# The opening of a macaron decoder layer: sums of squares by matmuls, modulation on ScalarE, weight parts on VectorE, seven conditioning rows at another place

## The chip, the cores and the metric

The kernel runs on one core of one Trainium2 chip. The metric is the time of one execution on the device in microseconds (us); of several executions the median is taken. The engines are TensorE (PE in the profile, its weight loads PEld), VectorE (DVE), ScalarE (ACT), GpSimd (POOL) and SyncE (SP), which here issues nearly all transfers.

## The reference

One layer, one sequence of 1024 tokens, width 1024, all in float32. Three sub-layers, each with a norm, a modulation by a conditioning vector c, and a gated residual:

```python
c_act = jax.nn.silu(c)
mods = jnp.split(c_act @ w_ada[l] + b_ada[l], 9, axis=-1)
sh1, sc1, gt1, sh2, sc2, gt2, sh3, sc3, gt3 = mods
h = modulate(rms_norm(x, g_ffn1[l]), sh1, sc1)      # h * (1 + scale) + shift
x = x + 0.5 * gt1[:, None, :] * swiglu(h, w1_gu[l], w1_down[l])
h = modulate(rms_norm(x, g_mix[l]), sh2, sc2)
...                                                 # gated convolution and windowed attention
h = modulate(rms_norm(x, g_ffn2[l]), sh3, sc3)
x = x + 0.5 * gt3[:, None, :] * swiglu(h, w2_gu[l], w2_down[l])
return rms_norm(x, g_final)
```

The feed-forward width is 2816, 22 blocks of 128. The change is in the first norm, its modulation and the first three of these blocks, and in when the rows of mods are made.

## The kernel before

Activations lie transposed: a tile holds 128 channels (db, 0 to 7) by 512 tokens (half h, 0 or 1). To keep float32 precision a product is three matmuls of operands split in a high part (the value rounded to the matmul format, written by ACT) and a low part (the rest, by subtraction): `mm3` issues high x high at L138, weight-high x activation-low at L140 and weight-low x activation-high at L142. `split` makes a weight's parts, cast at L106, subtraction at L107.

The opening, inside an order written out by hand for all engines, goes like this. The first half of x is loaded, 8 tiles. `Stats` squares each tile on ACT (L312, L315), adds the squares up on DVE (L319), and then four matmuls with a column of ones (L328) sum over the channels. `rstd_of` makes the inverse root, `spread` (L269) brings it to all partitions, and ACT copies it to sp (L642). Then eight steps, one for each db: DVE multiplies x by the norm and by the scale factor (L275), ACT adds the shift and rounds, giving the high part (L279), DVE makes the low part (L290), ACT writes the full value over x (L285). Between them stand the two rows of mods, shift and scale, that the next step needs: `ada_block` (L225) multiplies a 128 x 1024 block of w_ada by silu(c) and sums it on DVE, and `ada_done` (L235) makes g * (1 + scale). Six weight tiles (gate and up of blocks 0 to 2, w0[0] to w0[5]) are split meanwhile, their subtractions on POOL. `first_mm` issues the matmuls of a step with the tiles that are there. The second half of x gets the same sums, s1, during the last two steps, and then its own pass, `first_h`, with 144 matmuls behind it. That is the end of the hand-written order; PE's order is written out for the whole program.

Then `gu_seven` computes the other 19 blocks by a scheme with seven products in place of eight (L195), `down_seven` the down projection in 10 blocks with POOL adding into x, and the mixing stage follows. The other 56 rows of mods, `steps`, are taken by `some_ada`: seven ahead of `gu_seven`, one for each of its blocks, and the rest in the mixing stage. The order of DVE, ACT and SP outside the opening is set by a scheduler, and it put the seven rows among the sums of the second half. Weights and these rows are loaded through one ring of four buffers (wr, L114), and SP issues in order, so a load that waits for a buffer holds back those behind it.

## Time and profile before

| | |
|---|---|
| median of 3 runs | 2302.0 us (2300.78 to 2303.47) |
| the profiled execution | 2298.75 us, span 2296.8 |
| PE busy | 2210.1 us, 96% of the span |
| DVE busy | 1677.2 us, 73% |
| ACT busy | 1060.4 us, 46% |
| POOL busy | 394.4 us, 17% |

The span is what the profiler saw between the first and the last instruction. A row of the timeline gives start and length in us, engine, line, operation, what it writes and reads, how many of them were merged, and in brackets how long the engine had been idle and what ended that. A row of a group gives busy time and mean length in ns, and idle time before them. Lines are those of the kernel before; in the changed one they are about 10 to 60 higher.

### The profile page before, as it was taken

The numbers are of one execution on the slowest core, as the hardware profiler recorded it, in microseconds if no ns is written. First come the engines' busy times: TensorE is split into PE (matmuls) and PEld (weight loads), VectorE is DVE, ScalarE is ACT, GpSimd is POOL, SyncE is SP. The second block draws the span as 40 slices with busy tenths as digits, with TensorE's granted clock in tenths as the row PEclk, the third lists the DMA queues.
The fourth block names the chain that finished last, engine by engine and source line by source line (L and its number), as shares of the span: only waits on it lengthen the run. The fifth ranks groups of instructions, "written<-read, shape, count | busy, mean of one in ns | idle before, by whom it ended". The sixth has DMA issues, their size and how long they took to land.

```text
span 2296.8 us, 30100 instructions
## 1 busy us (share of the span) xinstructions
PE 2210.1 (96%) x10392; PEld 1849.1 (81%) x10392; DVE 1677.2 (73%) x2966; ACT 1060.4 (46%) x2095; POOL 394.4 (17%) x445
## 2 busy tenths in 40 slices
PE   5899999999998999999899997999999999999997
PEld 3688888888887888888889996788888888888886
DVE  8997778867868777777477776555786777676875
ACT  4554444444446443343476555124644444454442
POOL 3000000006451000000343442002100000002644
PEclk9999999999999999999999998999999999999998
DMA  8265456599732543454121115354233553399922
GB/s 319 76 220 180 149 176 211 193 404 297 262 121 97 183 131 109 155 156 156 55 64 56 52 44 217 131 177 149 69 124 121 184 185 122 119 342 335 351 79 74
DMA packets 146744, 381.63 MB, mean 166 GB/s; under 512 B 20384, under 2 KB 22560, under 8 KB 146592
## 3 DMA queue, kind: packets, MB, share of 16 engines
q1 hardware_dynamic: 141984, 371.33, 46.2%
q0 software_dynamic: 4608, 8.39, 2.1%
q8 instruction: 81, 1.33, 0.2%
q14 instruction: 71, 0.58, 0.1%
HBM read 270.61 MB, written 109.05 MB: 165 GB/s over the span
## 4 chain that ended last, share of the span: by engine, by line
PE 87%; DVE 7%; issue 2%; DMA 2%; ACT 2%; POOL 1%; SPq 0%; DVEq 0%; POOLq 0%; ACTq 0%
PE ps L195 60%; PE ps L142 6%; PE ps L138 6%; PE ps L140 6%; PE ps L977 2%; PE ps L975 2%; PE ps L976 2%; DVE w L107 1%; PE ps L1031 1%; PE ps L1074 1%; DVE t L225 1%; DMA wr<-in_w2d_dram 1%; DMA wr<-in_wada_dram 1%; PE ps L1010 1%; PE ps L1098 1%
## 5 line engine op out<-in xcount | busy, mean ns | idle before, releaser
L195 PE MATMUL ps<-t,w 128*128 128x512 f32 x6468 | 1469.1, 389 | 4.8 <-DVE r L405 3.6
L195 PEld LDWEIGHTS ps<-t,w 128*128 128x128 f32 x6468 | 1213.4, 188 | 260.1 <-DVE r L405 6.2
L106 ACT CAST w<-wr 128x512 fp32r<-128x512 f32 (+1 forms) x420 | 254.9, 612 | 482.4 <-PE ps L195 366.4
L107 DVE TENSOR_TENSOR w<-wr,w 128x512 fp32r<-128x512 f32 (+1 forms) x404 | 304.6, 760 | 137.8 <-ACT w L106 136.3
L515 POOL TENSOR_TENSOR x<-x,g 128x512 f32<-128x512 f32 x96 | 145.1, 1526 | 1060.1 <-DVE x L569 586.2
L106 ACT CAST w<-ws 128x512 fp32r<-128x512 f32 x231 | 143.5, 621 | 251.7 <-PE ps L195 202.1
L140 PE MATMUL ps<-t,w 128*128 128x512 f32 (+1 forms) x528 | 206.9, 392 | 4.9 <-DVE t L290 4.9
L107 DVE TENSOR_TENSOR w<-ws,w 128x512 fp32r<-128x512 f32 x231 | 161.7, 703 | 39.4 <-ACT w L106 38.9
L138 PE MATMUL ps<-t,w 128*128 128x512 f32 (+1 forms) x400 | 158.4, 396 | 6.3 <-ACT t L279 6.2
L142 PE MATMUL ps<-t,w 128*128 128x512 f32 (+1 forms) x400 | 155.9, 390 | 2.0 <-DVE w L107 2.0
L140 PEld LDWEIGHTS ps<-t,w 128*128 128x128 f32 x528 | 102.0, 193 | 27.1 <-DVE t L290 7.6
L344 DVE TENSOR_TENSOR x<-x,x 128x512 fp32r<-128x512 f32 x161 | 102.7, 685 | 2.9 <-ACT x L343 2.7
L343 ACT CAST x<-x 128x512 fp32r<-128x512 f32 x161 | 88.7, 621 | 19.4 <-DVE x L431 12.1
L225 DVE CUSTOM_DVE_ANT_0 wr<-wr,crow_act,v 128x1024 f32<-128x1024 f32 x56 | 71.7, 1282 | 35.1 <-DMA wr<-in_wada_dram 35.0
L138 PEld LDWEIGHTS ps<-t,w 128*128 128x128 f32 x400 | 78.1, 195 | 23.5 <-ACT t L279 9.0
L142 PEld LDWEIGHTS ps<-t,w 128*128 128x128 f32 x400 | 78.0, 195 | 17.3 <-DVE w L107 2.4
L107 POOL TENSOR_TENSOR w<-wr,w 128x512 fp32r<-128x512 f32 (+1 forms) x16 | 21.5, 1355 | 401.5 <-ACT w L106 401.5
L569 DVE SCALAR_TENSOR_TENSOR x<-ps,mods,x 128x512 f32<-128x512 f32 (+1 forms) x104 | 72.6, 707 | 23.9 <-PE ps L195 12.5
L319 POOL TENSOR_TENSOR s<-s,q 128x512 f32<-128x512 f32 (+1 forms) x48 | 56.7, 1184 | 192.1 <-ACT q L315 190.5
L975 PE MATMUL ps<-w,t 128*128 128x384 f32 x256 | 88.3, 345 | 0.0
L977 PE MATMUL ps<-w,t 128*128 128x384 f32 x256 | 85.7, 335 | 0.0
L976 PE MATMUL ps<-w,t 128*128 128x384 f32 x256 | 85.6, 334 | 0.0
(150 smaller groups left out, 2810.5 us busy)
## 6 DMA issues: line engine op xcount, KB each, us to landing
t<-hs SPq DMA_DIRECT2D x140, 512.0 KB, 9.8
hs<-x SPq DMA_DIRECT2D x277, 256.0 KB, 4.5
wr<-in_wada_dram SPq DMA_DIRECT2D x56, 512.0 KB, 3.7
wr<-in_w1gu_dram SPq DMA_DIRECT2D x44, 512.0 KB, 4.5
wr<-in_w2gu_dram SPq DMA_DIRECT2D x44, 512.0 KB, 3.6
wr<-in_wbcu_dram SPq DMA_DIRECT2D x24, 512.0 KB, 4.1
wr<-in_w1d_dram SPq DMA_DIRECT2D x22, 512.0 KB, 7.5
wr<-in_w2d_dram SPq DMA_DIRECT2D x22, 512.0 KB, 7.4
```

What stands on the lines that cost most here:

```text
L106: nc.scalar.copy(hi, src)
L107: lo_engine.tensor_tensor(lo, src, f32(hi), op=ALU.subtract)
L138: mm(o, wh, xh, start=start, stop=False)
L140: mm(o, wh, xl, start=False, stop=False)
L142: mm(o, wl, xh, start=False, stop=stop)
L195: mm(o, a, b, start=first, stop=last, skip_group_check=True)
L225: nc.vector.tensor_tensor_reduce(out=st, in0=st, in1=crow_act, scale=1.0, scalar=v[:, C_BADA + i : C_BADA + i + 1], op0=ALU.mult, op1=ALU. ...
L344: nc.vector.tensor_tensor(f32r(t), t, f32(hi), op=ALU.subtract)
L515: nc.gpsimd.tensor_tensor(dst, dst, r, op=ALU.add)
L975: mm(o[:, :384], xh, wh, start=k == 0, stop=False)
L976: mm(o[:, :384], xh, wl, start=False, stop=False)
L977: mm(o[:, :384], xl, wh, start=False, stop=k == KT - 1)
```

## The change

It does four things. First, the squares of each tile go to PE at once: `BankStats` has four matmuls with the column of ones for each of the eight tiles, adding up in PSUM, and DVE adds nothing. Second, DVE's product holds only the norm and the gain g, and ACT applies scale and shift in one operation, twice (rounded, and full over x); 1 + scale is made on ACT, and the low part is now full minus high. Third, the low parts of the six first weight tiles are made by DVE and not POOL, half a tile (512 columns) at a time, each half where it is first needed. Fourth, the seven rows ahead of `gu_seven` are not taken there, so each of the 56 moves seven places later, and `down_seven` takes one in each of its 10 blocks. Loads and matmuls are reordered to go with this.

```diff
+    class LateWeights(Weights):
+        def __init__(self, raw, tiles):
+            self.half, self.raw = HALF, raw
+            self.t = tiles or [parts_tile() for _ in range(2)]
+        def make(self, i):
+            split(*pair_of(self.t[i]), self.raw[:, i * HALF : (i + 1) * HALF])
...
+    class BankStats:
+        def __init__(self):
+            self.pt, self.n = None, 0
+        def add(self, src):
+            q = scratch("q")
+            nc.scalar.activation(q, src, AF.Square)
+            if self.pt is None:
+                self.pt = bank()
+            for b in range(NB // 2):
+                mm(self.pt[:, b : b + 1], q[:, b * P : (b + 1) * P], ones,
+                   start=self.n == 0 and b == 0, stop=True, skip_group_check=True)
+            self.n += 1
+        def rstd(self):
+            return rstd_of(self.pt[:, 0 : NB // 2], NB // 2, "n")
...
+        def first_u(db, h):
+            u = scratch("u")
+            nc.vector.scalar_tensor_tensor(
+                out=u, in0=xT[db][h], scalar=v[:, C_G1 + db : C_G1 + db + 1], in1=sp,
+                op0=ALU.mult, op1=ALU.mult,
+            )
+            return u
+        def first_hi(u, db, h):
+            for dst in (hh[db][h], xT[db][h]):
+                nc.scalar.activation(
+                    dst, u, AF.Identity, bias=mods[:, db : db + 1],
+                    scale=amod[:, db : db + 1],
+                )
+        def first_lo(db, h):
+            nc.vector.tensor_tensor(
+                hl[db][h], xT[db][h], f32(hh[db][h]), op=ALU.subtract)
...
             ada_block(crow_act, m, db, sta.pop(0))
             if m == 1:
-                ada_done(m, db, 1)
+                nc.scalar.activation(
+                    amod[:, db : db + 1], mods[:, 8 + db : 9 + db], AF.Identity, bias=ones)
...
-            u = modulated_hi(xT[db][0], sp, 0, db, hh[db][0])
+            first_hi(first_u(db, 0), db, 0)
             if db + 1 < KT:
                 first_ada(db + 1, 0)
-            modulated_lo(u, 0, db, hh[db][0], hl[db][0])
-            modulated_full(u, 0, db, xT[db][0])
+            first_lo(db, 0)
...
-        def first_w(i):
-            w0[i] = Weights(w0[i], 1024, nc.gpsimd, [tile_t(), tile_t()] if i > 3 else None)
+        def first_w(i, part):
+            if part == 0:
+                w0[i] = LateWeights(w0[i], [tile_t(), tile_t()] if i > 3 else None)
+            w0[i].make(part)
...
-        s0 = Stats(engine=nc.vector)
+        s0 = BankStats()
...
         first_step(7)
-        for db in range(2, KT):
+        s1 = BankStats()
+        for db in range(KT):
             s1.add(xT[db][1])
         first_mm((7,), 0, (0, 1, 2, 3, 4))
         r1 = s1.rstd()
...
-        some_ada(7)
         gu_seven(w1gu, range(3, NJ), hid, ts, lambda to: some_ada(1))
...
-        down_seven(w1d, hid, gate, ngate, xT, x_block)
+        down_seven(w1d, hid, gate, ngate, xT, x_block, lambda: some_ada(1))
```

What moves on the engines, at the three places that count. On PE at the start of the program (s and q are squares, nr the inverse root, t_113 the first channel block, w its weights), before:

```order
L328 MATMUL ps_267<-ones,s_219 128x1 x4
L269 MATMUL ps_292<-ident,nr_273 128x128 x4
L138 MATMUL ps_304<-t_113,w_283 128x512
L140 MATMUL ps_304<-t_113,w_283 128x512
L142 MATMUL ps_304<-t_113,w_283 128x512
L138 MATMUL ps_305<-t_113,w_298 128x512
```

and with the change:

```order
L355 MATMUL ps_221<-ones,q_219 128x1 x4
L355 MATMUL ps_221<-ones,q_226 128x1 x4
L355 MATMUL ps_221<-ones,q_232 128x1 x4
L355 MATMUL ps_221<-ones,q_238 128x1 x4
L355 MATMUL ps_221<-ones,q_244 128x1 x4
L355 MATMUL ps_221<-ones,q_250 128x1 x4
L355 MATMUL ps_221<-ones,q_256 128x1 x4
L355 MATMUL ps_221<-ones,q_262 128x1 x4
L279 MATMUL ps_313<-ident,nr_294 128x128 x4
L148 MATMUL ps_319<-t_113,w_304 128x512
L150 MATMUL ps_319<-t_113,w_304 128x512
```

One group of sums has become eight, one for each tile of squares. On DVE in the second step (u is the scaled block, t_244 to t_262 and t_278 to t_284 are rows of mods), before:

```order
L290 SCALAR_TENSOR_TENSOR t_113<-u_314,mods,t_113 128x512
L225 ISA t_252,mods<-t_252,crow_act,v 128x1024
L225 ISA mods 128x1
L235 SCALAR_TENSOR_TENSOR amod<-mods,v 128x1
L275 SCALAR_TENSOR_TENSOR u_338<-x_98,amod,spr_291 128x512
L225 ISA t_256,mods<-t_256,crow_act,v 128x1024
L225 ISA mods 128x1
L290 SCALAR_TENSOR_TENSOR t_114<-u_338,mods,t_114 128x512
```

and with the change, first DVE, then ACT beside it:

```order
L692 TENSOR_TENSOR t_113<-x_97,t_113 128x512
L235 ISA t_278,mods<-t_278,crow_act,v 128x1024
L235 ISA mods 128x1
L107 TENSOR_TENSOR w_333<-wr_274,w_333 128x512
L107 TENSOR_TENSOR w_343<-wr_280,w_343 128x512
L678 SCALAR_TENSOR_TENSOR u_351<-x_98,v,spr_312 128x512
L235 ISA t_282,mods<-t_282,crow_act,v 128x1024
L235 ISA mods 128x1
L692 TENSOR_TENSOR t_114<-x_98,t_114 128x512
```

```order
L686 ACTIVATE t_113<-u_325,mods,amod 128x512
L686 ACTIVATE x_97<-u_325,mods,amod 128x512
L705 ACTIVATE amod<-mods,ones 128x1
L106 CAST w_333<-wr_274 128x512
L106 CAST w_343<-wr_280 128x512
L686 ACTIVATE t_114<-u_351,mods,amod 128x512
L686 ACTIVATE x_98<-u_351,mods,amod 128x512
```

Weight subtractions (L107) have come between a row of mods and the next product, and the small product L235 on DVE has become L705 on ACT, ahead of the casts that these subtractions need. On PE near the end of the eight steps (t_119 and t_120 are the last two blocks, ps_564 and ps_543 the second half's sums, t_492 the sixth weight tile), before:

```order
L138 MATMUL ps_307<-t_120,w_359 128x512
L140 MATMUL ps_307<-t_120,w_359 128x512
L142 MATMUL ps_307<-t_120,w_359 128x512
L138 MATMUL ps_308<-t_120,t_395 128x512
L140 MATMUL ps_308<-t_120,t_395 128x512
L142 MATMUL ps_308<-t_120,t_395 128x512
L328 MATMUL ps_564<-ones,s_498 128x1 x4
L138 MATMUL ps_309<-t_113,t_492 128x512
L140 MATMUL ps_309<-t_113,t_492 128x512
L142 MATMUL ps_309<-t_113,t_492 128x512
```

and with the change:

```order
L148 MATMUL ps_323<-t_119,t_444 128x512
L150 MATMUL ps_323<-t_119,t_444 128x512
L152 MATMUL ps_323<-t_119,t_444 128x512
L355 MATMUL ps_543<-ones,q_541 128x1 x4
L355 MATMUL ps_543<-ones,q_548 128x1 x4
L355 MATMUL ps_543<-ones,q_554 128x1 x4
L355 MATMUL ps_543<-ones,q_560 128x1 x4
L355 MATMUL ps_543<-ones,q_566 128x1 x4
L355 MATMUL ps_543<-ones,q_572 128x1 x4
L355 MATMUL ps_543<-ones,q_578 128x1 x4
L355 MATMUL ps_543<-ones,q_584 128x1 x4
L148 MATMUL ps_319<-t_120,w_305 128x512
```

The 15 matmuls of t_120 stood ahead of the sums; now they stand behind all eight groups of them.

More of the change, by code (lines that the diff above doesn't have):

```diff
@@ L643, in first_spread @@
             return sp
+        def first_u(db, h):
[14 more added lines that the diff above has]
+                hl[db][h], xT[db][h], f32(hh[db][h]), op=ALU.subtract)
         def first_h(dbs, h):
-            us = [modulated_hi(xT[db][h], sp, 0, db, hh[db][h]) for db in dbs]
+            us = [first_u(db, h) for db in dbs]
             for u, db in zip(us, dbs):
-                modulated_lo(u, 0, db, hh[db][h], hl[db][h])
-            for u, db in zip(us, dbs):
-                modulated_full(u, 0, db, xT[db][h])
+                first_hi(u, db, h)
+            for db in dbs:
+                first_lo(db, h)
         def first_ada(db, m):
@@ L709, in tile_macaron_layer @@
         first_ada(0, 1)
-        first_w(0)
-        w0[4] = load_st(w1gu[2, 0])
+        first_w(0, 0)
+        first_ada_load(4)
         sp = first_spread(r0)
-        first_w(1)
         first = {(i, 0): bank() for i in range(6)}
-        first_ada_load(4)
         first_step(0)
+        first_w(1, 0)
         first_mm((0,), 0, (0, 1))
-        first_w(2)
+        first_w(2, 0)
         first_ada_load(5)
@@ L722, in tile_macaron_layer @@
         first_mm((0, 1), 0, (2,))
-        first_w(3)
+        first_w(3, 0)
         first_ada_load(6)
@@ L727, in tile_macaron_layer @@
         first_mm((0, 1, 2), 0, (3,))
-        first_w(4)
+        first_w(0, 1)
+        w0[4] = load_st(w1gu[2, 0])
         first_ada_load(7)
-        w0[5] = load_st(w1gu[2, 1])
         load_x(1)
@@ L733, in tile_macaron_layer @@
         first_mm((3,), 0, (0, 1, 2, 3))
+        first_w(1, 1)
+        first_w(4, 0)
+        w0[5] = load_st(w1gu[2, 1])
         first_mm((0, 1, 2, 3), 0, (4,))
         first_step(4)
-        first_mm((4,), 0, (0, 1, 2, 3, 4))
+        first_mm((4,), 0, (0, 1))
+        first_w(2, 1)
+        first_mm((4,), 0, (2,))
         first_step(5)
-        first_mm((5,), 0, (0, 1, 2, 3, 4))
-        first_w(5)
-        s1 = Stats(engine=nc.vector)
+        first_mm((5,), 0, (0, 1, 2))
+        first_w(3, 1)
+        first_mm((4, 5), 0, (3,))
         first_step(6)
-        for db in range(2):
-            s1.add(xT[db][1])
-        first_mm((6,), 0, (0, 1, 2, 3, 4))
+        first_w(4, 1)
+        first_mm((6,), 0, (0, 1, 2, 3))
+        first_mm((4, 5, 6), 0, (4,))
         first_step(7)
-        for db in range(2, KT):
+        s1 = BankStats()
+        for db in range(KT):
             s1.add(xT[db][1])
@@ L749, in tile_macaron_layer @@
         r1 = s1.rstd()
+        first_w(5, 0)
         first_sw(0, 0)
-        first_mm((0, 1, 2), 0, (5,))
+        first_w(5, 1)
+        first_mm((0, 1, 2, 3), 0, (5,))
         sp = first_spread(r1)
-        first_mm((3, 4, 5, 6, 7), 0, (5,))
+        first_mm((4, 5, 6, 7), 0, (5,))
         first.update({(i, 1): bank() for i in range(6)})
```

## The prediction

> **What bounds the kernel now.** I read the busy time by stage first, then TensorE's waits, then the timeline of the stage that the change touches. Columns of the first view: stretch and length, then busy time (instructions) of PE, PEld, DVE, ACT and POOL, granted PE clock, DMA share, GB/s.
>
> ```profile
> 20.00:30.00 10.00, 3.29 (x6) 1.78 (x6) 9.54 (x12) 4.46 (x8) 7.41 (x4) 1.00 1.03 410
> ...
> 60.00:70.00 10.00, 4.76 (x19) 3.11 (x17) 9.21 (x16) 4.46 (x8) 0.00 (x0) 0.98 0.53 160
> ...
> 80.00:90.00 10.00, 10.00 (x48) 8.36 (x48) 8.43 (x13) 6.78 (x11) 0.00 (x0) 1.00 0.01 2
> ...
> 540.00:560.00 20.00, 20.00 (x90) 16.55 (x89) 19.75 (x23) 8.31 (x14) 14.12 (x14) 1.00 1.02 314
> ```
>
> From 80 us PE is full, and still is at 540 to 560, in the first down projection. Before 80 us it is a third to a half busy and DVE is full. So the change is worth what it does to one moment: the end of the opening, after which PE has only work in a row. PE's waits up to 165 us agree; the third row is from the chain of waits:
>
> ```profile
> PE ps L328 <- DVE s L319: 22.3, 2, 13.7
> ...
> PE ps L195 <- DVE r L405: 0.7, 1, 0.7
> ...
> 116.74 13.37 PE ps L195 x59
> ```
>
> The two long ones stand before the group of matmuls that adds up each half's squares (13.7 and 8.6 us). I therefore follow the opening to the end of the second half's 144 matmuls: L195, the next stage, starts at 116.74 now. In a row a matmul takes 13.37 / 59 = 0.227.
>
> **Part 1, the first sums on TensorE.** Now:
>
> ```profile
> 6.56 0.61 ACT L312 ACTIVATE s<-x 128x512 f32<-128x512 f32 x1
> ...
> 8.30 3.98 ACT L315 ACTIVATE q<-x 128x512 f32<-128x512 f32 x6 [0.61 <-DMA x<-in_x_dram]
> ...
> 13.68 1.78 PEld L328 LDWEIGHTS ps<-ones,s 128*128 128x128 f32 x8 [13.68 <-DVE s L319]
> 13.69 1.87 PE L328 MATMUL ps<-ones,s 128*128 128x1 f32 x8 [13.69 <-DVE s L319]
> ...
> 15.59 0.26 ACT L253 ACTIVATE nt<-ps,eps 128x4 f32<-128x4 f32 x1 [2.01 <-PE ps L328]
> ...
> 16.36 0.16 DVE L259 TENSOR_TENSOR nt<-nt,nv 128x4 f32<-128x4 f32 x1
> 16.56 1.16 DVE L260 SCALAR_TENSOR_TENSOR nr<-nt,nr 128x4 f32<-128x4 f32 x1
> ...
> 20.57 0.75 DVE L275 SCALAR_TENSOR_TENSOR u<-x,amod,spr 128x512 f32<-128x512 f32 x1 [0.36 <-ACT spr L642]
> ```
>
> One group of four instructions runs as eight records with a fresh weight load each: 1.78 us for eight loads, about 0.213 apiece, 1.71 a group. The change removes seven DVE adds, but PE now does eight such groups instead of one. ScalarE delivers squares every 0.66 us, so PE is the slower: from 7.17 (6.56 + 0.61) it needs 8 x 1.71 = 13.7, to 20.9 instead of 15.56. **+5.3.** That is PE's slow clock; with the fast one a group costs:
>
> ```profile
> 688.10 1.05 PE L328 MATMUL ps<-ones,s 128*128 128x1 f32 x8 [0.31 <-POOL s L319]
> ```
>
> about 0.86 in a row. Does the burst itself raise the clock? Five stretches, cut where the granted clock changes in steps of about 3.41 us:
>
> ```profile
> 694.24:697.65 3.41, 3.41 (x10) 2.62 (x9) 3.26 (x5) 2.47 (x5) 0.21 (x1) 0.50 0.34 132
> 697.65:711.30 13.65, 8.87 (x39) 6.44 (x38) 13.64 (x17) 10.05 (x18) 5.01 (x3) 1.00 0.27 97
> 711.30:714.72 3.42, 3.42 (x11) 2.92 (x12) 0.73 (x5) 0.26 (x1) 0.00 (x0) 0.50 0.00 0
> 714.72:718.13 3.41, 3.41 (x9) 2.64 (x8) 0.00 (x0) 0.00 (x0) 0.00 (x0) 0.50 0.00 0
> 718.13:721.50 3.37, 3.37 (x20) 2.89 (x19) 0.00 (x0) 0.00 (x0) 0.00 (x0) 1.00 0.00 0
> ```
>
> In the first, third and fourth PE is busy without a gap at half clock. One such window of 512-column matmuls was enough to lift the clock at 697.65; the window from 711.30, whose first 0.8 us were one-column matmuls of this line, did not lift it, and it took the next one. So one-column matmuls count for less than they last, and a stretch of nothing else should stay slow: I take 20.9.
>
> The Trainium skill, "TensorE: Matmul & The Clock Gate", Part 1, says that whatever is issued in the first 3.4 us or so runs slow and everything after it fast, without asking which matmuls; by that the burst would end near 16.3. The window from 711.30 speaks against it.
>
> **Part 2, from the sums to the first block.** Now 15.56 to 20.57, 5.0 us, of which 1.0 is the last small DVE operation stretched by a running POOL subtraction (1.16 against the 0.16 before it). After: activation 0.3, five small DVE operations 0.9, then on ACT the scale's addition (behind ada row two: 1.3, itself near the 0.26 above), a 0.6 cast and the 0.6 copy of the spread, then DVE's half-tile subtraction 0.6: 4.1. **-0.9.** The first scaled block starts near 24.95.
>
> **Part 3, the eight steps.** An undisturbed step now, its ACT part and the last one's, a scale stretched by POOL, the prices of cast and subtraction; the second row is from the chain of waits, the last two are POOL's group and a load's time to land:
>
> ```profile
> 44.64 0.75 DVE L275 SCALAR_TENSOR_TENSOR u<-x,amod,spr 128x512 f32<-128x512 f32 x1
> ...
> 45.39 1.20 DVE t L225
> ...
> 45.43 0.73 ACT L279 ACTIVATE t<-u,mods 128x512 fp32r<-128x512 f32 x1 [2.72 <-DVE u L275]
> 46.06 0.71 ACT L285 ACTIVATE x<-u,mods 128x512 f32<-128x512 f32 x1
> ...
> 60.66 0.71 ACT L285 ACTIVATE x<-u,mods 128x512 f32<-128x512 f32 x1
> ...
> 48.70 0.75 DVE L275 SCALAR_TENSOR_TENSOR u<-x,amod,spr 128x512 f32<-128x512 f32 x1
> ...
> 33.59 1.73 DVE L275 SCALAR_TENSOR_TENSOR u<-x,amod,spr 128x512 f32<-128x512 f32 x1
> ...
> 36.60 1.12 ACT L106 CAST t<-wr 128x512 fp32r<-128x512 f32 x2
> ...
> 100.18 1.90 DVE L107 TENSOR_TENSOR t<-x,t 128x512 fp32r<-128x512 f32 x3
> ...
> L107 POOL TENSOR_TENSOR w<-wr,w 128x512 fp32r<-128x512 f32 x6 | 10.9, 1838 | 5.0 <-ACT w L106 5.0
> ...
> wr<-in_w1gu_dram SPq DMA_DIRECT2D x44, 512.0 KB, 4.5
> ```
>
> A step is 4.06 alone and about 6.0 with POOL at work; all, from 20.57 to the end of the last block's second ACT pass at 61.37, take 40.8. Taking the subtractions off POOL ends the stretching, worth about a microsecond in each of some ten DVE operations. The price: on DVE a step becomes scale 0.67, ada 1.2, low part 0.6, ada 1.2, weight subtraction 0.6, so 4.28. And two new waits. The low part now needs ACT's second pass: 0.75 + 0.62 + 0.72 from the scale's start against 0.67 + 1.2 of DVE work, 0.3 late. The weight subtraction needs a cast that stands on ACT behind the scale's addition, which needs the second ada row: 0.1 + 0.2 + 0.62, with hand-over 0.98, in which DVE does nothing and the next scale is queued behind. 5.56 a step. Six steps 33.3, two steps with a second subtraction 1.2, the last one with three sums of the next weights queued ahead 6.5, two ACT passes 2.1: 43.2. **+2.4** (bounds: no cast wait, -3.5; steps as long as the stretched ones, +5).
>
> The DMAs have slack. The fifth tile's load and with it the last ada pair and the second half of x wait on SP until the first tile's second subtraction has freed a buffer, near 24.95 + 3 x 5.56 + 0.6 = 42. They hold 3.7 MB, so 9 us at the 410 GB/s of the first view, and 4.5 us to land: there by 56; the ada pair is needed at 60 and the half at 68.
>
> **Part 4, the second sums and the seven rows.** Now, first one of DVE's groups between 61.4 and 73.7, then PE:
>
> ```profile
> L225 DVE CUSTOM_DVE_ANT_0 wr<-wr,crow_act,v 128x1024 f32<-128x1024 f32 x7 | 8.9, 1280 | 0.0
> ...
> 73.65 1.87 PE L328 MATMUL ps<-ones,s 128*128 128x1 f32 x8 [8.60 <-DVE s L319]
> 75.38 0.77 PE L138 MATMUL ps<-t,t 128*128 128x512 f32 x1
> ...
> 79.37 1.28 PE L269 MATMUL ps<-ident,nr 128*128 128x128 f32 x8
> 80.41 0.48 PE L138 MATMUL ps<-t,t 128*128 128x512 f32 x1
> ```
>
> The sums end at 75.38, 14.0 after the ACT pass (61.37), the seven rows' 8.4 us among them; both go from here. After: the first square is ready 0.6 behind the pass, at 68.7, and PE's eight groups follow: 6.9 at the fast clock. But they last over two of the 3.41 us windows, so one is filled with one-column matmuls alone; I take it that the clock falls, on average 5.1 us in, and the last 2.1 groups cost 1.71: 8.7, end at 77.4. 9.3 in place of 14.0: **-4.7** (-6.5 if the clock stays).
>
> **Part 5, what PE has left then.** The last block's 15 matmuls now come behind the sums and no more ahead of them: 39 before the second half and not 24, 15 x 0.227 = **+3.4.** Slow ones: today nine (75.38 to 79.37, a loss of 1.95); afterwards until a whole window is filled, 5.1 us on average, a loss of 2.55: **+0.6.** The second half's first low part follows the copy of the spread, two scales and two ACT passes (0.6 + 1.4 + 1.4), with only 12 matmuls, 2.7, as cover: **+0.7.**
>
> Sum: 5.3 - 0.9 + 2.4 - 4.7 + 3.4 + 0.6 + 0.7 = **+6.8 us**; PE would reach the next stage near 123.5 and not 116.7.
>
> **Part 6, the ten rows that land in the down projection.** 10 x 1.2 us DVE and ten loads in a stage with PE full. They cost nothing while the weights there stay ahead; what covers them is that a block's weights are prepared most of a block of 19 us ahead:
>
> ```profile
> 577.53 0.69 DVE L154 TENSOR_TENSOR ws<-wr,wr 128x512 f32<-128x512 f32 x1 [3.41 <-DMA wr<-in_w1d_dram]
> ...
> 601.92 0.75 DVE L569 SCALAR_TENSOR_TENSOR x<-ps,mods,x 128x512 f32<-128x512 f32 x1
> ```
>
> The first sum for a block's weights is at 577.5; its third product leaves PSUM at 601.9, so PE began it some 9.5 us (42 matmuls) before, near 592. DVE is at 19.75 of 20 in the stretch from 540: without that cover 1.2 to 2.3 each, at most about 20. I take 0; less than nothing is excluded, since PE has no wait there to remove. Three rows fewer in the mixing stage: 0, no wait of PE there names L225.
>
> The profiled execution took 2298.75 (span 2296.8), below the runs' median of 2302.0. Profile 2305.6, so the median **2309**.
>
> **Rivals.**
> A, the other side: **the burst raises the clock.** The squares' groups count as work, so the first burst speeds up after one window. Counted back 201 windows from 694.24, one runs from 8.17 to 11.58; by then 2.6 groups are done, and 5.4 at 0.86 end at 16.3 (+0.7). The second burst never slows (-6.5), and no slow matmuls follow it (-1.95). 0.7 - 0.9 + 2.4 - 6.5 + 3.4 - 1.95 + 0.7 = -2.2: 2300, no change. For it: the weight loads keep PE occupied (2.92 of 3.42 in the window from 711.30). Against: that window did not lift the clock. It decides if the first window that the burst fills lifts it.
> B, **slow at the start, fast at the second sums**: a one-column window is too weak to lift the clock but enough to hold it. 6.8 - 1.8 - 2.55 = +2.5: 2304.5, within the noise. The window 697.65 to 711.30 fell only after nearly 3 us of idleness.
> C, **DVE never waits for the casts** (-5.9) on top of A: 2294, faster. Against: the order on ACT puts the cast behind the addition in each step.
> D, **the down projection loses its cover**, +8 on the forecast: 2317. For it 19.75 of 20; against, a whole block of lead.
>
> **Chances.** Forecast 0.58, A 0.12, B 0.13, C 0.10, D 0.07. Under 0.2% (4.6 us) cannot be told from no change. Faster: C and a little of A, 0.13; same: the rest of A, B and the forecast's lower edge, 0.27; slower 0.60. Range 2298 to 2317, holding A, B and D; the forecast's own is 2304 to 2314.
>
> **What would show it.** Right: the 64 records of the first sums end near 21 and the first scale starts near 25; DVE idle about a microsecond before each L107; the second sums start near 69; granted clock 0.5 inside or right behind them; L205 starts near 123. Wrong: first sums done by 17, or L205 before 117; or new PE waits between 480 and 680.

## The result and the profile after

| | before | changed |
|---|---|---|
| median of 4 runs each | 2301.39 us (2297.54 to 2303.47) | 2314.83 us (2311.41 to 2318.73) |
| ratio of the times | | 1.0068, 95% interval 1.0056 to 1.0080 |
| the profiled execution's span | 2296.8 us | 2309.6 us |

The change makes the kernel 13.4 us slower by the medians, 13 to 18 us by the ratio's interval, where +7 was forecast. Two executions of kernels further down, of 3421 us (casts_first) and 7811 us (sums2_early), were slow ones and stand in no ratio. Cutting both profiled executions at the same four places shows where. The third and fourth columns are the times of a stage in us. (The next stage starts at 116.58 in the timeline of the kernel before; the prediction's 116.74 is the row of the chain.)

| from, to | how it is read | before | changed | difference |
|---|---|---|---|---|
| start, next stage | start of the first seven-product matmul | 116.58 | 127.13 | +10.55 |
| gate and up | to the first scaled copy `g<-ps` on ACT | 365.66 | 364.39 | -1.27 |
| down projection | to the end of its last seven-product matmul | 189.24 | 196.93 | +7.69 |
| all that follows | to the end of the span | 1625.3 | 1621.2 | -4.2 |

The last row is not the change's doing. In the sixteen profiles of this study that stretch takes 1621.2 to 1630.8 us, whatever was edited ahead of it, with slow windows of PE's clock at other places each time. So one profile's total is uncertain by some 5 us, and what an edit does is read from the cut at its own stage.

The busy time by stage of the changed kernel, in the stretches that the prediction showed (same columns: PE, PEld, DVE, ACT, POOL, granted PE clock, DMA share, GB/s):

```profile
20.00:30.00 10.00, 4.87 (x14) 3.23 (x14) 7.06 (x15) 4.50 (x9) 0.00 (x0) 1.00 1.03 410
60.00:70.00 10.00, 8.14 (x31) 5.66 (x31) 7.80 (x13) 4.65 (x8) 0.00 (x0) 0.93 0.35 105
80.00:90.00 10.00, 10.00 (x40) 8.47 (x40) 2.63 (x8) 3.16 (x5) 0.00 (x0) 0.73 0.20 52
540.00:560.00 20.00, 17.36 (x69) 13.62 (x69) 12.98 (x20) 6.51 (x11) 10.49 (x10) 0.91 0.84 206
```

The row at 80 to 90 is of the kind that was forecast: PE is full, but behind the second sums its clock is 0.73. The last row speaks against the forecast: at 540 to 560, in the first down projection, PE has lost 2.6 of 20 us although DVE, which was at 19.75, is now at 12.98: idle as well, not overworked. The timeline of the opening (start, length, engine, line, operation; in brackets the idle time before and what ended it; L355 are the one-column sums, L678 the scale, L692 the low part, L686 the pass on ACT, L205 the next stage):

```profile
6.43 13.81 PE L355 MATMUL ps<-ones,q 128*128 128x1 f32 x64 [6.43 <-ACT q L351]
...
24.32 0.75 DVE L678 SCALAR_TENSOR_TENSOR u<-x,v,spr 128x512 f32<-128x512 f32 x1
...
33.03 0.69 DVE L692 TENSOR_TENSOR t<-x,t 128x512 fp32r<-128x512 f32 x1 [0.45 <-ACT x L686]
...
35.80 0.69 DVE L107 TENSOR_TENSOR w<-wr,w 128x512 fp32r<-128x512 f32 x1 [0.87 <-ACT w L106]
36.41 0.74 DVE L678 SCALAR_TENSOR_TENSOR u<-x,v,spr 128x512 f32<-128x512 f32 x1
...
42.19 0.74 DVE L678 SCALAR_TENSOR_TENSOR u<-x,v,spr 128x512 f32<-128x512 f32 x1
...
68.41 0.80 ACT L686 ACTIVATE x<-u,mods,amod 128x512 f32<-128x512 f32 x1
...
69.78 12.14 PE L355 MATMUL ps<-ones,q 128*128 128x1 f32 x64 [0.91 <-ACT q L351]
...
127.13 8.10 PE L205 MATMUL ps<-t,w 128*128 128x512 f32 x35
```

The first sums take 13.81 us for 64 records, 0.216 each, slow to the end. From 36.41 to 42.19 is a step: 5.77 us, with DVE idle 0.45 before the low part and 0.87 before the weight subtraction. The second sums last 12.14 us. And in the down projection, PE's waits from 470 to 690 us (total, times, longest):

```profile
PE ps L205 <- DVE x L599: 2.1, 3, 1.2
PE ps L205 <- ACT w L106: 2.1, 1, 2.1
...
PE ps L205 <- DVE w L107: 0.5, 1, 0.5
```

The DVE and PE rows at the longest of them, in the timeline:

```profile
550.67 0.68 DVE L164 TENSOR_TENSOR ws<-wr,wr 128x512 f32<-128x512 f32 x1
...
552.05 0.73 PE L205 MATMUL ps<-t,w 128*128 128x512 f32 x2 [2.09 <-ACT w L106]
```

And a wait of SP's queue in the same stretch:

```profile
SPq L114 <- DVE mods L235: 37.6, 8, 11.6
```

and the same queue in the kernel before, from 460 to 672 us:

```profile
SPq L114 <- DVE w L107: 95.0, 19, 15.2
```

A block's first weight sum (L164) runs at 550.67, and 1.4 us later PE starts on what was cast from it, 2.09 us late. Before, PE had no such wait. SP waited for a buffer of the ring before as well, 95.0 us, but then for weights to be split; now 37.6 us of its waits are for conditioning rows to be used up before it can issue a load into their buffers.

### The profile page after: what moved, and what is told of

It reads as the page before. It is cut to its first block, busy times and chain, and to the rows that moved or that the text cites. A ratio compares the mean times of both kernels' runs of the same rounds, so it can differ in the third digit from the quotient of the medians.

```text
span 2309.6 us, 30301 instructions
## 1 busy us (share of the span) xinstructions
PE 2235.4 (97%) x10504; PEld 1870.6 (81%) x10504; DVE 1663.9 (72%) x2956; ACT 1065.0 (46%) x2103; POOL 376.4 (16%) x433
## 4 chain that ended last, share of the span: by engine, by line
PE 89%; DVE 4%; DMA 2%; ACT 2%; issue 2%; POOL 1%; SPq 0%; DVEq 0%; POOLq 0%; ACTq 0%
PE ps L205 62%; PE ps L152 6%; PE ps L150 6%; PE ps L148 6%; PE ps L1033 2%; PE ps L1035 2%; PE ps L1034 2%; PE ps L1089 1%; PE ps L1132 1%; DMA t<-in_wada_dram 1%; DVE w L107 1%; DMA x<-in_x_dram 1%; PE ps L1068 1%; PE ps L355 1%; PE ps L1156 1%
## 5 line engine op out<-in xcount | busy, mean ns | idle before, releaser
L205 PE MATMUL ps<-t,w 128*128 128x512 f32 x6468 | 1471.0, 389 | 7.1 <-DVE r L435 2.3
L205 PEld LDWEIGHTS ps<-t,w 128*128 128x128 f32 x6468 | 1214.3, 188 | 263.3 <-DVE r L435 4.2
L107 DVE TENSOR_TENSOR w<-wr,w 128x512 fp32r<-128x512 f32 (+1 forms) x412 | 308.5, 756 | 129.4 <-ACT w L106 128.0
L150 PE MATMUL ps<-t,w 128*128 128x512 f32 (+1 forms) x528 | 208.0, 394 | 6.8 <-DVE t L692 5.6
L107 DVE TENSOR_TENSOR w<-ws,w 128x512 fp32r<-128x512 f32 x231 | 164.6, 716 | 35.1 <-ACT w L106 34.7
L148 PE MATMUL ps<-t,w 128*128 128x512 f32 (+1 forms) x400 | 159.6, 399 | 6.3 <-ACT t L686 4.9
L150 PEld LDWEIGHTS ps<-t,w 128*128 128x128 f32 x528 | 102.5, 194 | 30.0 <-DVE t L692 9.0
L235 DVE CUSTOM_DVE_ANT_0 wr<-wr,crow_act,v 128x1024 f32<-128x1024 f32 x56 | 73.8, 1318 | 35.4 <-DMA wr<-in_wada_dram 35.2
L148 PEld LDWEIGHTS ps<-t,w 128*128 128x128 f32 x400 | 78.4, 196 | 24.1 <-ACT t L686 6.8
L595 ACT ACTIVATE g<-ps,mods 128x512 f32<-128x512 f32 x80 | 55.0, 687 | 57.6 <-PE ps L205 45.6
```

Source lines behind the costliest of these rows:

```text
L107: lo_engine.tensor_tensor(lo, src, f32(hi), op=ALU.subtract)
L148: mm(o, wh, xh, start=start, stop=False)
L150: mm(o, wh, xl, start=False, stop=False)
L205: mm(o, a, b, start=first, stop=last, skip_group_check=True)
```

## The experiments

All ratios are to the kernel before, run beside it on the same chip, with 95% intervals; the changed kernel's is 1.0068 (1.0056 to 1.0080). Where no other kernel is named, the edit is made to the changed kernel. The theory after the first look was that three costs add up: slow one-column matmuls in both sums, waits in the steps, and weights that come late in the down projection.

| run | first scale | next stage | down projection | ratio |
|---|---|---|---|---|
| before | 20.57 | 116.58 | 189.24 | 1 |
| changed | 24.32 | 127.13 | 196.93 | 1.0068 (1.0056 to 1.0080) |
| rows_only | 20.39 | 109.52 | 200.32 | 1.0019 (1.0011 to 1.0027) |
| rows_in_gu | 24.54 | 125.71 | 189.24 | 1.0041 (1.0030 to 1.0053) |
| ring5 | 24.83 | 129.20 | 189.24 | 1.0032 (1.0020 to 1.0044) |
| sums1_back | 19.44 | 122.22 | 197.69 | 1.0066 (1.0053 to 1.0079) |
| sums2_back | 24.54 | 120.28 | 197.67 | 1.0050 (1.0038 to 1.0062) |
| sums2_mixed | 24.95 | 125.10 | 197.40 | 1.0066 (1.0041 to 1.0090) |
| sums2_early | 24.79 | 119.98 | 196.94 | 1.0046 (1.0034 to 1.0057) |
| casts_first | 24.62 | 120.34 | 196.82 | 1.0060 (1.0036 to 1.0084) |
| low_parts_only | 20.28 | 116.56 | 189.24 | 0.9989 (0.9981 to 0.9998) |
| before_rows_gu | 20.58 | 111.02 | 189.24 | 0.9970 (0.9958 to 0.9982) |
| low_parts_casts | 19.01 | 108.35 | 189.24 | 0.9966 (0.9952 to 0.9979) |
| combined | 19.01 | 117.50 | 189.25 | 0.9975 (0.9965 to 0.9986) |
| early_all | 19.38 | 108.30 | 189.24 | 0.9958 (0.9945 to 0.9970) |
| wide_between | 36.83 | 139.61 | 197.45 | one run, 2328.4 us |

### The rows

**rows_only** edits the kernel before:

```diff
-        some_ada(7)
...
-        down_seven(w1d, hid, gate, ngate, xT, x_block)
+        down_seven(w1d, hid, gate, ngate, xT, x_block, lambda: some_ada(1))
```

> The kernel before with only the seven conditioning rows moved, as the change does (none ahead of the gate-and-up stage, one more after each block of the first down projection). Theory T (the moved rows alone make the down projection about 7.7 us longer, since the three loads of a block share four buffers and the sums of the next weights come late on DVE): from the first scaled copy to the last seven-product matmul of the down projection +6 to +9 us, new TensorE waits there for DVE or ACT. In the opening the second sums lose seven rows of 1.2 us ahead of them on DVE: TensorE's wait of 8.60 us before them shrinks, -4 to -7. Sum: 2300 to 2306. Rival R1 (the down projection got longer because everything arrives 10 us later than its transfers, not because of the rows): the down projection keeps its length, and the whole is 2294 to 2298.

The down projection takes 200.32, 11.1 us longer and above the 6 to 9 of the theory; R1 is out. The opening gains 7.06 us: the second sums start at 67.9 and not at 73.65. Together +4.0, and the ratio says +4.4 (0.19% of 2297). So the rows' move is two effects of opposite sign, and the good one is as large as the whole forecast.

**rows_in_gu** takes the rows elsewhere:

```diff
-        gu_seven(w1gu, range(3, NJ), hid, ts, lambda to: some_ada(1))
+        gu_seven(w1gu, range(3, NJ), hid, ts, lambda to: some_ada(2 if len(steps) > 42 else 1))
...
-        down_seven(w1d, hid, gate, ngate, xT, x_block, lambda: some_ada(1))
+        down_seven(w1d, hid, gate, ngate, xT, x_block)
```

> The changed kernel with the seven rows neither ahead of the gate-and-up stage nor in the down projection, but as a second row in its first seven blocks. T: the down projection gets back the length it had before (-7 us against the changed kernel), the gate-and-up stage pays 0 to 3 us for seven rows of 1.2 us on a DVE that is busy 78% there: 2306 to 2311. R1: as long as the changed kernel, 2313 to 2317.

The stage's first scaled copy and last products in the timelines, first of the changed kernel, then of this one:

```profile
491.52 0.69 ACT L595 ACTIVATE g<-ps,mods 128x512 f32<-128x512 f32 x1
...
639.73 48.72 PE L205 MATMUL ps<-t,w 128*128 128x512 f32 x213
```

```profile
490.10 0.69 ACT L595 ACTIVATE g<-ps,mods 128x512 f32<-128x512 f32 x1
...
639.73 39.62 PE L205 MATMUL ps<-t,w 128*128 128x512 f32 x173
```

639.73 + 39.62 - 490.10 = 189.25, within a hundredth of what it was before, against 196.93. The gate-and-up stage pays nothing: 364.39 in both. The ratio falls by 0.27%, 6.2 us.

**ring5** keeps the rows in the down projection and gives the ring a fifth buffer (two other pools give up one buffer each to make room; those lines are left out here):

```diff
-        st = wgt.tile([P, 1024], F32, tag="wr", name=nm("wr"), bufs=4)
+        st = wgt.tile([P, 1024], F32, tag="wr", name=nm("wr"), bufs=5)
```

> The changed kernel with five buffers and not four for the tiles into which weights and conditioning rows are loaded (and, to make room, seven scratch tiles and not eight, and one buffer for the negated gates). Theory T (three loads of a block share four buffers, so a load of the next weights waits for the sums of this block's, and DVE gets to them late): the down projection falls from 196.9 to 189 to 191 us, 2306 to 2309. Rival R4 (DVE is simply full there, ten rows of 1.3 us more than it can take): it stays at 195 to 200 us, the time within 2 us of the changed kernel.

189.24 again, with the same ten rows and the same work on DVE: R4 is out. PE's only wait from 470 to 690 us in this kernel is one that the kernel before has too:

```profile
PE ps L205 <- DVE r L435: 0.8, 1, 0.8
```

DVE's first sum for the weights of the same block (the fourth such sum from 455 us on) stands here in its timeline:

```profile
532.96 0.68 DVE L164 TENSOR_TENSOR ws<-wr,wr 128x512 f32<-128x512 f32 x1
```

and in the kernel before the stage's first scaled copy and the same sum here:

```profile
482.24 0.69 ACT L565 ACTIVATE g<-ps,mods 128x512 f32<-128x512 f32 x1
...
517.56 0.68 DVE L154 TENSOR_TENSOR ws<-wr,wr 128x512 f32<-128x512 f32 x1
```

Counted from the first scaled copy of the stage, that fourth sum runs at 59.1 us in the changed kernel (550.67 - 491.52), at 38.0 with five buffers (532.96 - 494.93), and at 35.3 with the rows in the other stage and in the kernel before (517.56 - 482.24). The 24 us between are more than a block of 19 us: the lead that the forecast had counted on. The loads set it, three a block in four buffers; the scheduler's order on DVE, which puts the sum behind the last products of the block ahead, goes with it and was not tried apart.

### The sums

**sums1_back** and **sums2_back** put one half's sum back on DVE:

```diff
-        s0 = BankStats()
+        s0 = Stats(engine=nc.vector)
```

```diff
-        s1 = BankStats()
+        s1 = Stats(engine=nc.vector)
```

> The changed kernel with the first half's sum of squares added up on DVE again (one group of one-column matmuls, not eight); the second half's stay on TensorE. T: the first sums end near 15.6 instead of 20.24, the first scale starts near 19.7 and the whole opening moves by -4.6 us: 2309 to 2311. Rival R2 (the first scale waits as well for the conditioning rows, the first weights or the clock, so that an earlier sum is worth little): first scale not before 22, 2313 to 2315.

> The changed kernel with the second half's sum of squares added up on DVE, all eight blocks behind the last step; the first half's stay on TensorE. T (eight slow groups on TensorE hold up 15 matmuls and the chain): DVE's adds end near 75.5, the sums near 77.4 instead of 81.8, and the 15 matmuls of the last block run ahead of them; the next stage starts near 120 instead of 127.1: 2306 to 2310. Rival R3 (the second half is late because its squares and its x come late, whoever adds them): the next stage within 2 us of 127, 2313 to 2317.

The first brings the first scale and the next stage 4.9 us forward, as the theory said; R2 is out at the landmark. In the time it cannot be seen (1.0066, the intervals overlap), with its down projection 0.8 and the rest 3 us longer in the profile. The second brings the next stage 6.85 us forward, and the time 0.18%, 4 us, with intervals that just overlap; R3 is out by the landmark. DVE's seven additions in a row beat PE's eight groups here: the sums end at 77.05 and not at 81.92, and the last block's 15 matmuls run meanwhile.

Why are the groups so slow? **sums2_mixed** leaves all as it is but for the order on PE:

```diff
         for db in range(KT):
             s1.add(xT[db][1])
-        first_mm((7,), 0, (0, 1, 2, 3, 4))
+            if db < 5:
+                first_mm((7,), 0, (db,))
```

> The changed kernel with the last block's 15 matmuls between the groups of the second sums, three behind each of the first five. Theory T (a stretch of nothing but one-column matmuls drops the clock; with 512-column matmuls between them it stays up): granted clock 1.00 through the sums, 64 records and 15 matmuls within 11 us, no slow matmuls behind, the next stage near 122 to 124: 2309 to 2312. Rival R6 (the clock falls there whatever stands between the groups, for instance because TensorE was half idle in the steps before): clock near 0.5 for 3.4 us or more behind 72 us, next stage 126 to 128, 2313 to 2317.

PE's timeline, a group among 512-column matmuls, then the last three groups in a row and what follows:

```profile
73.67 0.95 PE L355 MATMUL ps<-ones,q 128*128 128x1 f32 x8
74.48 0.47 PE L148 MATMUL ps<-t,w 128*128 128x512 f32 x1
...
78.43 3.00 PE L355 MATMUL ps<-ones,q 128*128 128x1 f32 x24
82.29 0.80 PE L148 MATMUL ps<-t,t 128*128 128x512 f32 x1 [0.86 <-ACT t L106]
82.89 0.63 PE L150 MATMUL ps<-t,t 128*128 128x512 f32 x1
```

Mixed, a group takes 0.81 us and the clock stays up from 70.4 to 80.7; three groups follow alone from 78.4, 3.00 us, and the matmuls behind them are slow until 87.6. So a stretch of nothing but one-column matmuls brings the clock down, and R6 is out for the mixed part. The next stage came only 2.0 us sooner, not 3 to 5: the slow matmuls are still there, only later, and PE then waits 0.86 us for a cast.

**sums2_early** spreads the groups over the steps:

```diff
         first_mm((4, 5), 0, (3,))
+        s1 = BankStats()
+        for db in range(2):
+            s1.add(xT[db][1])
...
         first_mm((6,), 0, (0, 1, 2, 3))
+        for db in range(2, 5):
+            s1.add(xT[db][1])
         first_mm((4, 5, 6), 0, (4,))
         first_step(7)
-        s1 = BankStats()
-        for db in range(KT):
+        for db in range(5, KT):
             s1.add(xT[db][1])
```

> The changed kernel with the second half's squares and their groups of one-column matmuls earlier: two blocks behind the sixth step, three behind the seventh, three behind the eighth. Theory T (the groups cost what they cost because they stand in a row on the path; in the steps TensorE is half idle and would take them for nothing): the second sums end near 73 instead of 81.8, the next stage near 117 to 119 instead of 127.1, 2305 to 2308. Rival R7 (ScalarE is then late with the scale-and-shift passes, and one-column matmuls in a half idle stretch drop the clock earlier): the last pass 2 us or more later, next stage 122 to 127, 2310 to 2315.

```profile
62.83 1.84 PE L355 MATMUL ps<-ones,q 128*128 128x1 f32 x16
...
67.35 2.73 PE L355 MATMUL ps<-ones,q 128*128 128x1 f32 x24
...
72.12 2.73 PE L355 MATMUL ps<-ones,q 128*128 128x1 f32 x24
```

All 64 records now run fast, 24 of them in 2.73 us, 0.114 each, and the sums end at 74.7 and not at 81.8. The next stage starts at 119.98, 7.15 us sooner, a little short of the theory's 117 to 119; the steps are no later (the last scale is 42.5 us behind the first, as in the changed kernel), so R7 is out. One window after the last groups is still slow, 75.2 to 78.6.

**wide_between** asks whether the first sums could be sped up by company:

```diff
...
+            if wide:
+                mm(wide, ident, q, start=True, stop=True)
...
```

> The changed kernel with one more matmul behind each group of the first sums: 512 columns of the same squares against the identity into a bank that nobody reads (added work). Theory T (one-column matmuls alone do not lift the clock, matmuls with 512 columns among them do): granted clock 1.00 before 16 us, the 64 records and the eight wide matmuls done by 17 to 22. Rival R11 (the clock cannot be lifted this early whatever TensorE does; in both kernels it went up only at 35 to 37 us): half clock until after 25 us, the burst ends at 27 to 35.

PE's timeline (L355 the groups, L358 the added matmul, L150 and L148 those of the steps):

```profile
8.47 2.06 PE L358 MATMUL ps<-q,ident 128*128 128x512 f32 x2
10.31 1.71 PE L355 MATMUL ps<-ones,q 128*128 128x1 f32 x8
...
32.36 2.05 PE L358 MATMUL ps<-q,ident 128*128 128x512 f32 x2
...
50.29 0.63 PE L150 MATMUL ps<-t,w 128*128 128x512 f32 x1
...
51.15 0.43 PE L148 MATMUL ps<-t,w 128*128 128x512 f32 x1
```

The theory fails here: PE is occupied without a gap from 6.7 to 34.2, half of the time with 512 columns, and stays slow. R11 has the burst's end right (34.2). No fixed time after the start lifts the clock; that nothing can lift it before some time is not excluded, as no run fills a window with 512-column matmuls before 27.8. It rises at 51.15 here, at 35.3 before and at 37.4 in the changed kernel, which is 14.3, 14.7 and 13.0 us behind the first scale each time. Here that is the end of the first row of the steps' own matmuls without a gap, from 46.3 on. Whether the added ones, plain float32 and two records each, count less than the steps' own is not shown: they fill 1.85 us of each 3.41, and the first window that the steps' own fill to the end, 47.8 to 51.2, lifts the clock.

### The steps

**casts_first** moves each cast ahead of the addition for the next scale, on ACT:

```diff
-        def first_step(db):
+        def first_step(db, *ws):
             first_hi(first_u(db, 0), db, 0)
+            for i, part in ws:
+                if part == 0:
+                    w0[i] = LateWeights(w0[i], [tile_t(), tile_t()] if i > 3 else None)
+                w0[i].cast(part)
             if db + 1 < KT:
                 first_ada(db + 1, 0)
...
+            for i, part in ws:
+                w0[i].rest(part)
```

> The changed kernel with each cast of a first weight's half tile on ScalarE straight behind the two scale-and-shift passes of its step, ahead of the scale's addition; nothing else moves. Theory T (DVE idles 0.87 us in each step because the cast stands behind the addition, which needs the second conditioning row): no wait of DVE for a cast, a step of 4.9 and not 5.77 us, seven steps: the last pass 6 us earlier, the next stage near 121 instead of 127.1, 2306 to 2310. Rival R5 (a step is held by something else, the low part that waits for the second pass, or the loads of the last rows): steps stay above 5.5 us, 2312 to 2316.

DVE's waits from 20 to 70 us, of the changed kernel and of this one:

```profile
DVE w L107 <- ACT w L106: 6.1, 7, 0.9
DVE t L692 <- ACT x L686: 4.7, 8, 1.6
```

```profile
DVE t L701 <- ACT x L695: 3.5, 8, 0.4
DVE w L147 <- ACT w L143: 0.9, 1, 0.9
```

Six of the seven waits for a cast are gone, a step takes 4.81 us (29.98 to 34.79), and the next stage comes 6.8 us sooner, so R5 is out. Not all of it is the casts': from the first scale to the last, 42.5 us become 35.4, of which six steps give 0.96 each, 5.8 in all, and the last step 1.3, because there two sums of later weights (1.2 us) now stand behind the scale on DVE and no more ahead of it. The time, 1.0060 with a wide interval, did not settle what that is worth. **low_parts_casts** does: of two kernels with both sums on DVE and the rows in the gate-and-up stage, **low_parts_only** has the casts where the change put them, **low_parts_casts** has them ahead.

> The changed kernel with both sums added up on DVE again and the seven rows in the first blocks of the gate-and-up stage, so that of the change only scale and shift on ScalarE and the first weights' low parts on DVE are left. T: next stage at 127.1 - 4.9 (first sums) - 6.9 (second sums) = 115.4, about 6 us later than the kernel before with the same rows (109.5): these two parts alone cost 6 us, the whole 2295 to 2299 where before takes 2297. Rival R9 (without the rows and the slow groups the steps are no longer than before's, since no DVE operation is stretched by GpSimd): next stage at or below 109.5, 2288 to 2292.

> Both sums on DVE, the seven rows in the gate-and-up stage, and each cast ahead of the scale's addition. Theory T (the waits for the casts are a cost of their own, 0.87 us a step, whatever adds the squares up): next stage at 116.6 - 6.8 = 109.8 and the time 7 us below that of the same kernel with the casts behind, ratio to before 0.996. Rival R12 (the time does not follow the opening: with the casts moved alone it fell by some 2 us while the next stage came 6.8 us sooner): next stage near 110, but a ratio of 0.998 or more.

From the first scale to the next stage low_parts_only takes 96.3 us (116.56 - 20.28) and low_parts_casts 89.3, and the ratio goes from 0.9989 to 0.9966, with intervals that do not meet: the next stage comes 8.2 us sooner, 7.0 of them in this stretch (some 1.3 again by the two sums behind the last scale), 5.3 arrive in the time, and R12 is out. In **before_rows_gu**, the kernel before with the same rows and nothing else changed, the stretch takes 90.4. So the new way of scaling and of making low parts costs 5.8 us where the change put the casts, and R9 is out; with the casts ahead it is 1.1 us better than what it replaced, which the ratios (0.9966, 0.9970) cannot tell apart.

### What beats both

**before_rows_gu** is one edit to the kernel before, the rows as in rows_in_gu.

> The kernel before with only the seven rows moved, each as a second row in one of the first seven blocks of the gate-and-up stage. Theory T (what was good in the change is that seven rows no longer stand ahead of the second sums; what was bad in it comes from its other parts and from the down projection's loads): next stage at 109.5 as with the rows moved to the down projection, down projection 189.2, gate-and-up 0 to 2 us longer: 5 to 7 us faster than before, 2290 to 2293 where before takes 2297. Rival R8 (the seven rows cost on DVE what they cost, wherever they stand): within 2 us of before.

0.9970, 7 us faster, as the theory said; R8 is out. Two kernels then put all the better parts together (first sums on DVE, casts ahead, rows in the gate-and-up stage) and differ in where the second half's one-column groups stand: three behind the seventh step and five among the last matmuls (**combined**), or two, three and three as in sums2_early (**early_all**).

> The changed kernel with the first sums on DVE, each cast ahead of the scale's addition, the second half's squares three behind the seventh step and five behind the last with the last block's matmuls between their groups, and the seven rows in the first blocks of the gate-and-up stage. T (the gains of the separate runs add up): first scale 19.4, steps of 4.81, last pass near 58, next stage 127.1 - 4.9 - 6.8 - 7.1 = 108.3, 2288 to 2292 where before takes 2297. Rival R10 (with everything earlier the second half's x, loaded through the same queue, is the next thing late): TensorE or ScalarE waits for x, next stage 111 to 116, 2293 to 2298.

> First sums on DVE, casts ahead of the scale's addition, seven rows in the gate-and-up stage, and the second half's squares and one-column groups two behind the sixth step, three behind the seventh and three behind the last. Theory T (groups of one-column matmuls among the steps' 512-column matmuls do not drop the clock for more than a window or two): next stage 108 to 111, ratio 0.995 to 0.997. Rival R13 (with the steps shorter the one-column groups are a larger share of TensorE's work, and once the clock has fallen the mixture does not lift it, as in the run with three and five groups, where it stayed at half for 20 us): next stage 115 to 118, ratio 0.998 to 1.000.

PE's timeline of combined:

```profile
55.03 2.73 PE L364 MATMUL ps<-ones,q 128*128 128x1 f32 x24
...
60.92 1.70 PE L364 MATMUL ps<-ones,q 128*128 128x1 f32 x8
62.48 0.77 PE L157 MATMUL ps<-t,w 128*128 128x512 f32 x1
...
72.86 1.70 PE L364 MATMUL ps<-ones,q 128*128 128x1 f32 x8
```

In this profile the clock fell at 58.5, behind three groups in a row, and then the mixture that held it up in sums2_mixed did not bring it back: it rose at 79.0, behind 512-column matmuls alone. Its next stage, 117.50, is in no theory's favour: it lies above both T's 108.3 and R10's 111 to 116, and x was there in time. The median of its runs (2290.4, 2287.6 to 2301.3) is lower than this profile's span of 2299.4, so most executions seem not to fall into it. early_all does not fall for longer than a window (64.3 to 67.7), reaches the next stage at 108.30, as T said, and has the lowest ratio of the study: 0.9958, 2289.4 us where before takes 2298.2. It, low_parts_casts, combined and before_rows_gu beat both kernels; their intervals overlap. early_all and low_parts_casts differ only in where the second half's squares are added up, and reach the next stage at 108.30 and 108.35: at the best place found for them, the sums by matmuls are no faster in these profiles than those on DVE.

## Why the prediction was right and wrong

The direction was right. The size was not, because a term that was set to nothing cost 7.7 us and one in the opening was mis-sized by 3.3. By the prediction's own terms:

| term | forecast | measured | from |
|---|---|---|---|
| Part 1, first sums | +5.3 | +4.7 | end 20.24, was 15.56 |
| Part 2, to the first scale | -0.9 | -0.9 | 4.08, was 5.01 |
| Part 3, eight steps | +2.4 | +4.1 | 24.32 to 69.21, 44.9, was 40.8 |
| Part 4, second sums and rows | -4.7 | -1.4 | 69.21 to 81.78, 12.6, was 14.0 |
| Part 5, what PE has left | +4.7 | +4.1 | 81.78 to 127.13, 45.3, was 41.2 |
| Part 6, down projection | 0 | +7.7 | 196.93, was 189.24 |
| not forecast | | -5.4 | gate and up -1.3, the rest of the span -4.2 |
| sum of the spans | +6.8 | +12.8 | |

**Parts 1, 2 and 5** came out within 0.7 us. (The first burst began 0.7 us sooner than forecast and lasted as long; in Part 5 the slow matmuls were eight, fewer than the nine of before and not more.) The first burst did not lift the clock, so rival A is out, and B and C with it: the second burst did not stay fast, and DVE waits for the casts.

**Part 3** found both waits, and the forecast 0.98 for the cast was 0.87. A step became 5.77 and not 5.56: each of its two rows of mods takes 1.28 with the short read that ends it, and not 1.2, and the low part is 0.45 late and not 0.3. That wait is the pass on ACT: taken as 0.72 with a shift alone, it takes 0.81 with a scale operand as well, and there are two of them ahead of the low part. The Trainium skill, "ScalarE: Activation LUTs", section "What ACT_TABLE_LOAD costs", gives about 93 ns for each such operand; the rows agree (0.73 to 0.81), and that sentence would have sharpened the term. What the waits for the casts cost shows in casts_first.

**Part 4** is the larger miss in the opening, 3.3 us. That the clock falls in the burst was right; "on average 5.1 us in" was not. At 0.114 fast and 0.213 slow, 64 records in 12.0 us mean that some 17 ran fast: it fell 1.9 us in. PE's busy time and granted clock, cut at the window in which the burst begins:

```profile
68.24:71.65 3.41, 2.50 (x20) 1.00 0.38 137
71.65:75.07 3.42, 3.42 (x18) 0.50 0.02 5
```

In the five other kernels with this burst (10.65 to 12.58 us) the granted clock falls 1.4 to 3.5 us in, so always sooner than the forecast's mean. The forecast let the burst fill a window of its own first. But the window in which it begins already counts: here it holds 0.6 us of 512-column matmuls, 0.9 us of idleness and then the burst. In all six the fall stands at the end of the first window of which the burst takes more than a tenth of a microsecond.

**Part 6** is the step that failed. It took 0 from the cover "a block's weights are prepared most of a block of 19 us ahead", read from a profile in which no rows were loaded in that stage. But the rows come through the same ring of four buffers as the weights, as the description of the kernel before says, and three loads a block leave no room for a block's lead: the edit removes the cover on which its price was set to nothing. DVE at 19.75 of 20 was the wrong worry: with five buffers the same work on DVE costs nothing. Rival D named the place and, with 8 us, the size, for the reason of a full DVE, and was given a chance of 0.07. Of the 7.7 us, PE's waits make up 4.8 (2.09, 0.55 and three for DVE), and a slow window of 3.4 us behind the first of them, at 552.9 to 556.3, another 1.6 or so; the last 1.3 were not traced. The prediction's own sign of being wrong is what appeared: "new PE waits between 480 and 680".

What the prediction did not set apart is that the move of the rows is worth 5.6 to 7.1 us in the opening when nothing takes its place: before_rows_gu and rows_only reach the next stage at 111.0 and 109.5. The forecast has it inside Part 4, netted against the slow burst.

## What to carry to other kernels

Work that is moved takes its loads along: before its price in the new place is set to nothing, count the buffers of every ring that it passes through there, and ask whether the lead that hides it survives one more load a block. A reduction by one-column matmuls belongs among wider matmuls, a few at a time, and not in a row ahead of the work that waits for it; even so it was no faster here than the additions on DVE. On an engine that works in order, put what another engine needs soon ahead of what itself has to wait.

## What was not expected of the hardware

One-column matmuls are paid twice. 64 in a row keep a slow clock slow for 13.8 us (0.216 each), and bring a fast one down after 1.9 us here; the 512-column matmuls behind them then take 0.427 and not 0.227 for another 3.5 us (81.78 to 85.3).

The clock has a memory: eight one-column and three 512-column records in turn held it up for 8 us in sums2_mixed (70.4 to 78.4) and did not lift it in 15 us in combined (60.9 to 75.9). And being occupied is not enough: 27 us without a gap, half of it matmuls of 512 columns, did not lift it in wide_between. The Trainium skill, "TensorE: Matmul & The Clock Gate", Part 1, has the clock rise after one busy window of some 3.4 us whatever is issued; combined, wide_between and both bursts of the changed kernel disagree with that, and the changed kernel agrees with the length of a window (slow stretches of 3.4 us at 552.9 and at 58.0).

What goes with each change can be read from the traces. The granted clock changes on a grid of 3.41 us (in the changed kernel at 58.00, 61.41, 71.65 and 85.31). In the windows of that grid over the first 105 us of the sixteen profiles, a slow clock rose behind every window with 2.91 us or more of 512-column matmuls (42 windows) and behind none with 2.85 or less (181); a fast one fell behind every window with less than 1.5 and behind none with 2.0 or more. The mixtures of wide_between and combined held at most 1.85 and 2.44 us in a window, so they need no other reason. The figures are those of the opening: at one place between 1440 and 1490 us, each profile has a window with 2.9 to 3.2 us that did not lift the clock.

In all these profiles the granted clock reads 1.00 from the start up to the first fall, while the records before 31 us or later have the slow length. For the opening, the length of a record tells the clock, and the column does not.
